# Hybrid HGRN2/Mamba-2 block on one core: the lower parts of 18 weight blocks are made in the stage of step sizes and fetched from DRAM

## The chip, the core and the metric

The kernel runs on 1 core of one Trainium2 chip. The metric is the device time of one execution in microseconds (us), lower is better. Before the change it takes 2316.17 us, the median of 3 runs (2312.27 to 2316.66).

## The reference, cut to what matters

One layer of a hybrid block: a modulated layer norm, two token mixers that read the same input through one combined projection, gates and an output projection, then a feed-forward part. All arrays are float32, with 1024 positions and a width of 1024.

```python
mod = (cond @ w_ada[l] + b_ada[l])[:, None, :]
sh1, sc1, g1, sh2, sc2, g2 = jnp.split(mod, 6, axis=-1)
u = layer_norm(x) * (1.0 + sc1) + sh1
proj = u @ w_in
q, f, i, g, z, xbc, dt, gate_a, gate_b = jnp.split(proj, offs, axis=-1)
y_a = hgrn2_mixer(q, f, i, g, lb, gnorm) @ w_branch_a
y_b = mamba2_mixer(z, xbc, dt, conv_w, conv_b, dt_bias, a_log, d_skip, ssm_norm) @ w_branch_b
...
# in mamba2_mixer
xbc = jax.nn.silu(causal_dwconv(xbc, conv_w, conv_b)).astype(F32)
delta = jax.nn.softplus(dt.astype(F32) + dt_bias.astype(F32)).reshape(bsz, s, B_GROUPS, B_HG)
```

The change concerns the columns of w_in that give xbc: 2048 of x and 4 groups of 128 each for B and C. In the kernel these are 24 weight blocks of 1024 x 128.

## The kernel before, in words

**Two-part products.** A float32 value is split into an upper part (the value cast to a shorter float type, held in 4 bytes) and a lower part (the value less the upper part). A product is three matmuls into the same PSUM bank (`mm`, L80 to L83): lower weights by upper input or the other way round, and upper by upper. The input u stays in SBUF as `uh` and `ul`, in two halves of 512 positions.

**Weight blocks.** `Dense.load` (L67) makes the two parts of one block of 128 x 1024 numbers (512 KB): a transfer on SP's queue into `raw` (L70), a cast to `wh` on ScalarE (L75, called ACT in the profile) and a subtraction to `wl` (L76) on the engine `dn.lo`. That engine is VectorE (DVE) by default and GpSimd (POOL) in the mixers, since `dn.lo = G` is set ahead of each. The tiles `raw`, `wh` and `wl` have two slots each in the pool `wp`, and w_i's pieces (`iraw`) use the slots of `raw` too. So a load waits for the cast and the subtraction of the load two before it, and a `wl` can be written again when TensorE (PE) has ended the block two before. `Dense.unit` (L85) does a block: 2 halves x 8 slices x 3 matmuls, 48 in all, with a bank that is read out after each half.

**Stages around the change.** The stage of step sizes (357 to 467 us) multiplies u by w_i, the 1056 columns of dt and i, in three groups of 352 columns; a group is 8 tiles of 128 positions with 24 matmuls each. Its weights come in four pieces a group (`load_i`, L565) that are split into `iwh` (ScalarE) and `iwl` (VectorE). Beside that it makes four more segments of the modulation (`mod_segment`): 32 pieces `wa` of w_ada (512 KB, L213, three slots) are multiplied by the condition and summed on VectorE into `acc` (L215, L217), and PE reduces `acc` over partitions: 8 products with a column of ones (L222) for two segments, 2 row products (L231) for the other two. `Fill` lets a generator advance to a given step; `mods.to(...)` spreads the 36 steps of the segments over the 24 tiles. `step_sizes` makes delta and its sums on VectorE and ScalarE, and writes them to DRAM as `ac_d`.

Then come the HGRN2 mixer (467 to about 800 us) and the Mamba-2 mixer, in this document "the mixer" (to 1263 us). In the mixer four groups of 8 chunks follow one another. While the chunks of a group are worked on, `dense_x` (L811 on) makes the projection of the next group by `fill`: blocks B, C and 4 blocks of x, each followed by the convolution over 4 taps on VectorE (L832 on full rows, L835 on the 3 columns at an edge). Gate blocks follow behind the last group. A chunk fetches `ac` (L850) and `eb` (L860) from `ac_d`; the group before is normalised by `squares` (it fetches `zs`, L943, multiplies on GpSimd, L944, squares on ScalarE, L946, sums on VectorE, L948) and `finish` (stores `yb_d`, L964).

**What sets the order.** The program's text gives the order in which work is asked for; a scheduler then orders the instructions of each engine by its own estimate of when their operands are ready. Each engine works through its own queue strictly in that order. All transfers named here are issued by one queue, SP's: one that waits (for a slot, or for the data that it stores) holds all behind it.

Of the kernel before, what the change touches and what calls it, by code (L numbers as in the profile page):

```python
# [9 lines left out]
F32 = mybir.dt.float32  # L10
# [22 lines left out]
P = 128  # L33
T = 1024
TT = T // P
# [15 lines left out]

B_Q, B_F, B_G, B_Z, B_X, B_B, B_C, B_GA, B_GB = 0, 8, 16, 24, 40, 56, 60, 64, 72
NBLK = 80

C_CT, C_BADA, C_CW, C_CB, C_DS, C_NW, C_GN, C_LB = 0, 8, 56, 152, 176, 192, 208, 209
NCOL = 225
# [4 lines left out]
class Dense:  # L61
# [2 lines left out]
    def __init__(self, tc, pool, psum):  # L64
        self.nc, self.pool, self.psum, self.lo = tc.nc, pool, psum, tc.nc.vector

    def load(self, src, scale=None, into=None, eng=None):  # L67
        nc = self.nc
        raw = self.pool.tile([P, 1024], F32, tag="raw", name="raw")
        nc.sync.dma_start(out=raw, in_=src)  # L70
        if scale is not None:
            r2 = raw.rearrange("p (k n) -> p k n", k=2)
            nc.vector.tensor_tensor(r2, r2, scale[:, None, :].broadcast_to([P, 2, TH]), op=ALU.mult)
        wh, wl = into or [self.pool.tile([P, 1024], F32R, tag=t, name=t) for t in ("wh", "wl")]
        nc.scalar.copy(wh, raw)  # L75
        (eng or self.lo).tensor_tensor(wl, raw, wh.bitcast(F32), op=ALU.subtract)  # L76
        return wh, wl

# [4 lines left out]
        nc.tensor.matmul(ps, sh, mh, start=False, stop=last)  # L83

    def unit(self, src, uh, ul, evac, ths=(0, 1), fine=False):  # L85
        wh, wl = src if isinstance(src, (tuple, list)) else self.load(src)
        wh = wh.rearrange("p (k n) -> p k n", k=KT)
        wl = wl.rearrange("p (k n) -> p k n", k=KT)
        for th in ths:
            ps = self.psum.tile([P, TH], F32, tag="d", name="dps")  # L90
            for kt in range(KT):
                self.mm(ps, wh[:, kt, :], wl[:, kt, :], uh[th][:, kt, :], ul[th][:, kt, :],
                        kt == 0, kt == KT - 1)
                if fine and kt < KT - 1:
                    yield
            evac(th, ps)
            yield
# [18 lines left out]
def chain(*gens):  # L116
    for g in gens:
        yield from g
# [3 lines left out]
def hybrid_block(ctx, tc, x, w_mod, w_ada, w_blk, w_i, w_ba, w_bb, w_o, w_g, w_u, w_d,  # L122
                 cols, masks, rows, hrows, out):
    nc = tc.nc
# [6 lines left out]
    def act(o, i, func, **k):  # L131

        if table_of[func] != tables[0]:
            tables[0] = table_of[func]
            r = S.preload_act_table_set(tables[0])
            tc.stamp_issue_order_token(r.ins, "act_tables")
        r = S.activation(o, i, func, **k)
        tc.stamp_issue_order_token(r.ins, "act_tables")
# [11 lines left out]
    z_d = tc.dram_tile([16, P, T], F32, name="z_d")  # L150
    h_d = tc.dram_tile([NFT, P, T], F32, name="h_d")
    x1_d = tc.dram_tile([TT, P, D], F32, name="x1_d")

    mk = const.tile([P, NMASK, P], F32, name="mk")
    cl = const.tile([P, NCOL], F32, name="cl")
# [34 lines left out]
    def split(hi, lo, src, eng=G):  # L190
        S.copy(hi, src)  # L191
        eng.tensor_tensor(lo, src, hi.bitcast(F32), op=ALU.subtract)  # L192
# [11 lines left out]
    uh = [bigp.tile([P, KT, TH], F32R, tag="big", name=f"uh{i}") for i in range(2)]  # L204
    ul = [bigp.tile([P, KT, TH], F32R, tag="big", name=f"ul{i}") for i in range(2)]
# [32 lines left out]
    dn = Dense(tc, wp, psd)  # L238

    def gate_evac(which, n, logs=False):  # L240
        dst = (ga_d, gb_d)[which]

        def evac(th, ps):
            sg = wp.tile([P, TH], F32, tag="ge", name="ge")
            if logs:
                act(sg, ps, AF.Exp, scale=-1.0)
                act(sg, sg, AF.Ln, bias=ones[:, 0:1])
                act(sg, sg, AF.Exp, scale=-1.0)
            else:
                act(sg, ps, AF.Sigmoid)  # L250
            nc.sync.dma_start(out=dst[n, :, TH * th:TH * th + TH], in_=sg)
        return evac

    def gate_units(which, n0, n1, fine=False, ths=(0, 1)):
        for n in range(n0, n1):
            yield from dn.unit(w_blk[(B_GA, B_GB)[which] + n], uh, ul, gate_evac(which, n, fine), ths, fine=fine)
# [16 lines left out]
    with tc.tile_pool(name="sw", bufs=1) as sw, tc.tile_pool(name="s0p", bufs=2, space=PSUM) as pp:  # L273
# [176 lines left out]
        for q in range(len(pairs)):  # L450
            blk = pairs[q][0]
# [104 lines left out]
    with tc.tile_pool(name="s1", bufs=2, reuse_waits="tile") as sp, \  # L556
            tc.tile_pool(name="s1p", bufs=2, space=PSUM, reuse_waits="tile") as pp:
        mods = Fill(chain(mod_segment(4, sp, pp, col=3), mod_segment(3, sp, pp, col=2),
                          mod_segment(2, sp, pp, row=0), mod_segment(5, sp, pp, row=1)))
        NI = 352  # L560
        iraw = []

        def load_i(g, k4):
            raw = wp.tile([P, 1024], F32, tag="raw", name="iraw")[:, 0:2 * NI].rearrange("p (k n) -> p k n", k=2)
            nc.sync.dma_start(out=raw, in_=w_i[g, :, 2 * k4:2 * k4 + 2, :])  # L565
            return raw

        bridge = dn.load(w_blk[B_GA + 6])
        iraw = [load_i(0, k4) for k4 in range(2)]
        for g in range(3):  # L570
            wh = sp.tile([P, KT, NI], F32R, tag="iwh", name="iwh")
            wl = sp.tile([P, KT, NI], F32R, tag="iwl", name="iwl")
            for k4 in range(4):
                ks = slice(2 * k4, 2 * k4 + 2)
                raw = iraw.pop(0) if iraw else load_i(g, k4)
                split(wh[:, ks, :], wl[:, ks, :], raw, V if IE[k4] == "V" else G)
            if g == 0:
                for _ in dn.unit(bridge, uh, ul, gate_evac(0, 6), (1,)):
                    pass
                lower_bound()  # L580
            for tt in range(TT):
                ps = psd.tile([P, TH], F32, tag="d", name="dps")
                th, o = tt // 4, P * (tt % 4)
                for kt in range(KT):
                    dn.mm(ps[:, 0:NI], uh[th][:, kt, o:o + P], ul[th][:, kt, o:o + P], wh[:, kt, :], wl[:, kt, :],
                          kt == 0, kt == KT - 1)
                S.copy(i_sb[:, tt, NI * g:NI * g + NI], ps[:, 0:NI])
                mods.to((TT * g + tt + 1 - MO) * 36 / (24 - MO))
                if g == 1 and tt == 4:
                    steps.drain()  # L590
            if g == 0:
                steps = Fill(step_sizes(sp, pp))
                steps.to(1)
        mods.drain()


    def hgrn_phase():
# [208 lines left out]
    def mamba_phase():  # L806
        with tc.tile_pool(name="m", bufs=2, reuse_waits="tile") as mp, \
# [3 lines left out]
            def dense_x(g):  # L811
# [6 lines left out]
                for blk, dst in [(16 + g, bT), (20 + g, cT)] + [(4 * g + j, xT[:, j, :]) for j in range(4)]:  # L818
# [22 lines left out]
                                act(t, t, AF.Silu, bias=cl[:, C_CB + k:C_CB + k + 1])  # L841
                            held[:] = held[1:] if len(held) == 2 and not th else []

                    yield from dn.unit(w_blk[B_X + blk], uh, ul, evac, fine=True)

            def fetch(g, ch):

# [135 lines left out]
            for i in range(N):  # L983
                g, ch = divmod(i, TT)
# [31 lines left out]
    with tc.tile_pool(name="big2", bufs=4, reuse_waits="tile") as big2:  # L1016
        with tc.tile_pool(name="dp", bufs=2, reuse_waits="tile") as dp, \
# [40 lines left out]
            for i, (o, n) in enumerate(steps):  # L1058
                if n == 0:
                    fill = Fill(operand(o + 1) if o < 2 else first_operands())  # L1060
                wh, wl = (t.rearrange("p (k n) -> p k n", k=KT) for t in w)
# [157 lines left out]
        with tc.tile_pool(name="fp", bufs=2, reuse_waits="tile") as fp, \  # L1219
# [139 lines left out]
            for p in range(2):  # L1359
# [10 lines left out]
                into = [None] * 2  # L1370
                if p:
                    ht = [pool.tile([P, 4, 2, TH], F32R, tag=t, name="htl") for pool, t in ((bigp, "big"), (big2, "big2"))]
                    wt = [big2.tile([P, 2, 2, D], F32R, tag="big2", name="wtl") for _ in range(3)]
                    into = [(ht[q // 4][:, q % 4], (wt[q // 2][:, q % 2, 0, :], wt[q // 2][:, q % 2, 1, :])) for q in range(NL)]
# [93 lines left out]
```

## Time and profile before

| | |
|---|---|
| median of 3 runs | 2316.17 us |
| the profiled execution | 2310.18 us |
| its span (first to last instruction) | 2308.4 us |
| mean granted clock of TensorE | 0.988 |
| bytes moved by DMA | 290.75 MB, mean 126 GB/s |

The profile is of one execution. Its first page gives, for each engine, the busy time and its share of the span. Further views list, for a window of time, the busy time of each engine, the clock that TensorE was granted and the load of the 16 DMA engines; for a group of instructions, their number, duration and the idle time ahead of them; for an engine, the waits and what ended each (its releaser). A row of a timeline has the start, the duration, the engine, the line, the operation and, in brackets, the idle time just before it and its releaser. "SPq" is SP's queue of transfers. Matmuls overlap, so one takes longer than the distance from one start to the next.

### The profile page before, as it was taken

To read this page: it belongs to the slowest core of one execution; us is meant where nothing else is said; L and a number is where in the kernel's file an instruction comes from. 1 tells how busy PE (TensorE), PEld (TensorE's weight loads), DVE (VectorE), ACT (ScalarE), POOL (GpSimd) and SP (SyncE) were. 2 spreads that over 40 slices of the span, in tenths; PEclk is the share of its full clock that TensorE was granted. 3 is DMA by queue.
4 is the path that set the end of the run, shared out by engine and by line. 5 is a ranking of instruction groups with operands and counts; after the bars stand their busy time and mean duration, and the time that the engine had idled before them with its cause. 6 is when DMAs were issued, how large, how long until landed. Compare 5 with 4: busy or idle time off the path is not lost.

```text
span 2308.4 us, 32125 instructions
## 1 busy us (share of the span) xinstructions
PE 2230.2 (97%) x12412; PEld 1816.2 (79%) x12412; DVE 1567.8 (68%) x2489; ACT 1061.6 (46%) x1931; POOL 264.8 (11%) x153
## 2 busy tenths in 40 slices
PE   7899999999999999999998999999899999999998
PEld 4778889977777787787776788888788888888886
DVE  5866665638898558898975443468977666653647
ACT  3833333137777646777786320224633333322221
POOL 0000000012222222222231000003400000000000
PEclk9999999999999999999999999999999999999999
DMA  7334326601112312343455643432232222244554
GB/s 282 121 140 136 126 93 209 218 33 52 61 56 69 118 61 92 110 141 115 159 164 183 229 167 102 132 138 95 73 132 101 87 73 92 73 160 151 179 182 132
DMA packets 119649, 290.75 MB, mean 126 GB/s; under 512 B 12101, under 2 KB 26949, under 8 KB 119497
## 3 DMA queue, kind: packets, MB, share of 16 engines
q1 hardware_dynamic: 119496, 288.71, 37.5%
q8 instruction: 97, 1.59, 0.3%
q14 instruction: 56, 0.45, 0.1%
HBM read 235.05 MB, written 53.62 MB: 125 GB/s over the span
## 4 chain that ended last, share of the span: by engine, by line
PE 82%; DVE 8%; ACT 3%; issue 3%; DMA 2%; POOL 2%; SPq 0%; DVEq 0%; POOLq 0%; ACTq 0%
PE dps L81 11%; PE dps L83 11%; PE dps L82 11%; PE fps L81 9%; PE fps L82 9%; PE fps L83 9%; PE dqs L81 4%; PE dqs L83 4%; PE dqs L82 4%; PE hps L83 1%; PE hps L81 1%; PE hps L82 1%; PE sc_ps L701 1%; DVE xTm L832 1%; PE yi L918 1%
## 5 line engine op out<-in xcount | busy, mean ns | idle before, releaser
L81 PE MATMUL dps<-uh,wl 128*128 128x512 f32 x800 | 331.7, 415 | 3.3 <-POOL wl L76 3.3
L83 PE MATMUL dps<-uh,wh 128*128 128x512 f32 x800 | 316.5, 396 | 0.0
L82 PE MATMUL dps<-ul,wh 128*128 128x512 f32 x800 | 314.8, 393 | 0.0
L76 POOL TENSOR_TENSOR wl<-raw,wh 128x1024 fp32r<-128x1024 f32 x49 | 132.1, 2696 | 790.4 <-ACT wh L75 723.4
L81 PEld LDWEIGHTS dps<-uh,wl 128*128 128x128 f32 x800 | 155.1, 194 | 37.6 <-issue 6.6
L83 PEld LDWEIGHTS dps<-uh,wh 128*128 128x128 f32 x800 | 151.9, 190 | 33.8
L82 PEld LDWEIGHTS dps<-ul,wh 128*128 128x128 f32 x800 | 152.5, 191 | 26.7
L81 PE MATMUL dqs<-yp,wl 128*128 128x512 f32 x384 | 147.5, 393 | 6.6 <-ACT yp L191 4.3
L82 PE MATMUL dqs<-yp,wh 128*128 128x512 f32 x384 | 150.4, 392 | 0.0
L83 PE MATMUL dqs<-yp,wh 128*128 128x512 f32 x384 | 150.1, 391 | 0.0
L179 POOL TENSOR_TENSOR mv<-mv,kc 128x1 f32<-128x1 f32 x32 | 32.3, 1015 | 1026.7 <-DVE mv L178 1023.5
L191 ACT CAST cw<-raw 128x512 fp32r<-128x512 f32 x131 | 81.0, 621 | 132.3 <-PE fps L83 87.6
L81 PE MATMUL fps<-t,cw 128*128 128x512 f32 x352 | 137.0, 389 | 0.7 <-DVE cw L192 0.7
L82 PE MATMUL fps<-t,cw 128*128 128x512 f32 x352 | 136.9, 389 | 0.0
L83 PE MATMUL fps<-t,cw 128*128 128x512 f32 x352 | 136.9, 389 | 0.0
L75 ACT CAST wh<-raw 128x1024 fp32r<-128x1024 f32 x76 | 79.6, 1048 | 113.5 <-PE dqs L83 101.8
L192 DVE TENSOR_TENSOR cw<-raw,cw 128x512 fp32r<-128x512 f32 x131 | 94.8, 725 | 43.5 <-ACT cw L191 42.2
L82 PE MATMUL fps<-wl,hp 128*128 128x512 f32 x304 | 118.4, 389 | 0.0
L83 PE MATMUL fps<-wh,hp 128*128 128x512 f32 x304 | 118.3, 389 | 0.0
L192 DVE TENSOR_TENSOR wl<-wdr,wh 128x1024 fp32r<-128x1024 f32 x38 | 46.5, 1224 | 105.4 <-ACT wh L191 105.2
L81 PE MATMUL fps<-wh,hp 128*128 128x512 f32 x304 | 117.0, 390 | 0.5 <-ACT wh L191 0.5
L191 ACT CAST wh<-wdr 128x1024 fp32r<-128x1024 f32 x38 | 40.1, 1054 | 147.4 <-PE fps L83 146.1
(368 smaller groups left out, 5586.4 us busy)
## 6 DMA issues: line engine op xcount, KB each, us to landing
raw<-in_w_blk_dram SPq DMA_DIRECT2D x79, 512.0 KB, 3.4
wdr<-in_w_d_dram SPq DMA_DIRECT2D x44, 512.0 KB, 3.8
wa<-in_w_ada_dram SPq DMA_DIRECT2D x32, 512.0 KB, 4.5
ac<-ac_d SPq DMA_DIRECT2D x32, 512.0 KB, 4.8
raw<-in_w_g_dram SPq DMA_DIRECT2D x26, 512.0 KB, 3.8
raw<-in_w_u_dram SPq DMA_DIRECT2D x26, 512.0 KB, 3.5
hr<-h_d SPq DMA_DIRECT2D x44, 256.0 KB, 3.9
h_d<-sg SPq DMA_DIRECT2D x18, 512.0 KB, 2.9
```

Of the source, the lines that this page charges most:

```text
L75: nc.scalar.copy(wh, raw)
L76: (eng or self.lo).tensor_tensor(wl, raw, wh.bitcast(F32), op=ALU.subtract)
L81: nc.tensor.matmul(ps, sl, mh, start=first, stop=False)
L82: nc.tensor.matmul(ps, sh, ml, start=False, stop=False)
L83: nc.tensor.matmul(ps, sh, mh, start=False, stop=last)
L179: G.tensor_tensor(mv[:, 2:3], mv[:, 1:2], kc[:, 2:3], op=ALU.pow)
L191: S.copy(hi, src)
L192: eng.tensor_tensor(lo, src, hi.bitcast(F32), op=ALU.subtract)
L701: PE.matmul(sp_[b0:b1, 0, b1:b2], lv[c][:, o + b0:o + b1], lv[c][:, o + b1:o + b2], start=True, stop=True)
L832: V.scalar_tensor_tensor(d[:, o:], ps[:, o + j - 3:TH + j - 3], cw(j), d[:, o:], op0=ALU.mult, op1=ALU.add)
L918: PE.matmul(yi[64 * e:64 * e + 64, j, :], xd[:, HP * hh:HP * hh + HP], ac[:, hh, :], start=True, stop=True)
```

## The change

`AHEAD` lists 18 blocks: B, C and the four x of groups 1, 2 and 3. `make_lower` is a generator that loads each of them in the stage of step sizes, splits it (on VectorE there, since `dn.lo` is V) and stores the lower part in the DRAM tile `wl_d`; the store of one block is asked for after the next block's load. A `Fill` spreads the 19 steps over the tiles of the stage's first 22. In the mixer `weights` gives `Dense.unit` a function for these blocks: it loads `raw` and casts it as before, and fetches `wl` from `wl_d` on SP's queue in place of the subtraction. The upper part is not kept. Line numbers move: L70 becomes L71, L76 becomes L80, L213 becomes L218, L565 becomes L587.

```diff
+AHEAD = [b for g in range(1, 4) for b in [B_B + g, B_C + g] + [B_X + 4 * g + j for j in range(4)]]
...
-    def load(self, src, scale=None, into=None, eng=None):
+    def load(self, src, scale=None, into=None, eng=None, lower=None):
...
         nc.scalar.copy(wh, raw)
+        if lower is not None:
+            nc.sync.dma_start(out=wl.bitcast(F32), in_=lower)
+            return wh, wl
         (eng or self.lo).tensor_tensor(wl, raw, wh.bitcast(F32), op=ALU.subtract)
...
-        wh, wl = src if isinstance(src, (tuple, list)) else self.load(src)
+        wh, wl = src() if callable(src) else src if isinstance(src, (tuple, list)) else self.load(src)
...
+    wl_d = tc.dram_tile([len(AHEAD), P, 1024], F32, name="wl_d")
...
+    made = {}
+
+    def weights(blk):
+
+        return (lambda: dn.load(w_blk[blk], lower=wl_d[made[blk]])) if blk in made else w_blk[blk]
+
+    def make_lower(blks):
+
+        last = None
+        for blk in blks + [None]:
+            wl = dn.load(w_blk[blk])[1] if blk is not None else None
+            if last:
+                made[last[0]] = len(made)
+                nc.sync.dma_start(out=wl_d[made[last[0]]], in_=last[1].bitcast(F32))
+            last = blk, wl
+            yield
...
+        lower = Fill(make_lower(AHEAD))
         for g in range(3):
...
                 mods.to((TT * g + tt + 1 - MO) * 36 / (24 - MO))
+                lower.to((TT * g + tt) * (len(AHEAD) + 1) / 22)
...
         mods.drain()
+        lower.drain()
...
-                    yield from dn.unit(w_blk[B_X + blk], uh, ul, evac, fine=True)
+                    yield from dn.unit(weights(B_X + blk), uh, ul, evac, fine=True)
```

The scheduler decides where the new transfers stand. SP's queue at the start of the stage of step sizes, before (`wa`: a piece of w_ada, `iraw`: a piece of w_i, `hr`: constants of the step sizes; the number behind a name is that of the buffer):

```order
L213 DMA wa_2965<-in_w_ada_dram 128x1024
L516 DMA hr_3032<-in_hrows_dram 128x64
L213 DMA wa_2994<-in_w_ada_dram 128x1024
L213 DMA wa_2997<-in_w_ada_dram 128x1024
L213 DMA wa_3026<-in_w_ada_dram 128x1024
L213 DMA wa_3029<-in_w_ada_dram 128x1024
L565 DMA iraw_3059<-in_w_i_dram 128x704
L565 DMA iraw_3063<-in_w_i_dram 128x704
```

And after, from about the same place on (`raw`: a block's load, `wl_d`: the store of a lower part):

```order
L218 DMA wa_2990<-in_w_ada_dram 128x1024
L71 DMA raw_2852<-in_w_blk_dram 128x1024
L71 DMA raw_2884<-in_w_blk_dram 128x1024
L218 DMA wa_2993<-in_w_ada_dram 128x1024
L218 DMA wa_3029<-in_w_ada_dram 128x1024
L272 DMA wl_d_73<-wl_2855 128x1024
L71 DMA raw_2917<-in_w_blk_dram 128x1024
L272 DMA wl_d_73<-wl_2887 128x1024
L71 DMA raw_2957<-in_w_blk_dram 128x1024
L218 DMA wa_3032<-in_w_ada_dram 128x1024
```

Loads and stores of the blocks now stand among the pieces of w_ada; the pieces of w_i for the second group come after seven loads and six stores.

At the end of the stage SP's queue held the following before; the four `raw` are the first weights of the HGRN2 mixer:

```order
L70 DMA raw_3659<-in_w_blk_dram 128x1024
L213 DMA wa_3234<-in_w_ada_dram 128x1024
L213 DMA wa_3237<-in_w_ada_dram 128x1024
L70 DMA raw_3717<-in_w_blk_dram 128x1024
L70 DMA raw_3779<-in_w_blk_dram 128x1024
L70 DMA raw_3886<-in_w_blk_dram 128x1024
L213 DMA wa_3325<-in_w_ada_dram 128x1024
```

Behind these stood 15 more `wa`. After the change the last `wa`, the last store and the same first weights are:

```order
L71 DMA raw_3664<-in_w_blk_dram 128x1024
L272 DMA wl_d_73<-wl_3628 128x1024
L218 DMA wa_3697<-in_w_ada_dram 128x1024
L218 DMA wa_3700<-in_w_ada_dram 128x1024
L272 DMA wl_d_73<-wl_3667 128x1024
L218 DMA wa_3730<-in_w_ada_dram 128x1024
L218 DMA wa_3733<-in_w_ada_dram 128x1024
L232 DMA br_3763<-in_rows_dram 1x1024
L71 DMA raw_3786<-in_w_blk_dram 128x1024
L71 DMA raw_3844<-in_w_blk_dram 128x1024
```

The first weights of the HGRN2 mixer have moved from the middle of the `wa` to behind the last of them.

In the mixer SP's queue held, for about two chunks before (`yb_d`: the store of a group's result; `ac`, `eb`, `zs`: operands of chunks and of the normalisation):

```order
L964 DMA yb_d<-xTm 128x512 x4
L850 DMA ac<-ac_d 128x1024
L70 DMA raw<-in_w_blk_dram 128x1024
L943 DMA zs<-z_d 128x512
L860 DMA eb<-ac_d 64x4x128 x2
L850 DMA ac<-ac_d 128x1024
L943 DMA zs<-z_d 128x512 x3
```

And at the same place after:

```order
L989 DMA yb_d<-xTm 128x512 x4
L875 DMA ac<-ac_d 128x1024
L78 DMA wl<-wl_d 128x1024
L71 DMA raw<-in_w_blk_dram 128x1024
L968 DMA zs<-z_d 128x512
L885 DMA eb<-ac_d 64x4x128 x2
L875 DMA ac<-ac_d 128x1024
L968 DMA zs<-z_d 128x512 x3
```

A fetch of `wl` now stands ahead of the load of `raw`, behind an `ac`.

## The prediction, made before the changed kernel was run

> **What bounds the kernel now.** I read the first page, then busy time by stages, then TensorE's waits in the mixer.
>
> ```profile
> span 2308.4 us, 32125 instructions
> PE 2230.2 (97%) x12412; PEld 1816.2 (79%) x12412; DVE 1567.8 (68%) x2489; ACT 1061.6 (46%) x1931; POOL 264.8 (11%) x153
> ```
>
> PE (TensorE) is busy for 97%, so all its idle time is 78.2 us. A change that adds no matmul can win only some of these, or add to them. The stages that the change touches (columns: window, length, busy time of each engine, clock, DMA share, GB/s):
>
> ```profile
> 357.00:467.00 110.00, 107.80 (x658) 102.31 (x656) 62.78 (x79) 26.69 (x47) 5.22 (x2) 1.00 0.64 212
> 861.00:1059.00 198.00, 190.20 (x1083) 151.11 (x1083) 172.44 (x287) 147.41 (x313) 45.02 (x23) 0.99 0.37 116
> 1059.00:1157.00 98.00, 93.58 (x523) 73.66 (x520) 89.48 (x144) 74.39 (x156) 26.85 (x14) 0.98 0.41 137
> 1157.00:1263.00 106.00, 99.57 (x558) 77.51 (x556) 73.91 (x106) 77.79 (x170) 26.21 (x13) 0.97 0.52 168
> ```
>
> The first row is the stage of step sizes: PE is idle for 2.2 of 110 us, and the DMA moves 212 GB/s at share 0.64, the most of these rows. The others are the mixer from its second group on, idle for 7.8, 4.4 and 6.4 us. TensorE's waits there, by line and releaser (total, times, longest):
>
> ```profile
> PE trx L871 <- ACT xTm L137: 7.4, 2, 4.0
> PE dps L81 <- POOL wl L76: 3.3, 2, 2.4
> PE yi L918 <- ACT csh L191: 3.2, 1, 3.2
> PE yx L910 <- DVE Sm L927: 3.0, 2, 2.5
> ```
>
> Only 3.3 us are waits for a lower part itself. The two waits of trx have the same subtraction some steps back. One of them in order of time:
>
> ```profile
> 1037.90 3.45 POOL L76 TENSOR_TENSOR wl<-raw,wh 128x1024 fp32r<-128x1024 f32 x1 [13.70 <-ACT wh L75]
> 1039.77 1.61 DVE L835 SCALAR_TENSOR_TENSOR xTm<-edge,cl,xTm 128x3 f32<-128x3 f32 x1
> 1041.96 0.20 DVE L835 SCALAR_TENSOR_TENSOR xTm<-edge,cl,xTm 128x3 f32<-128x3 f32 x1
> 1045.40 0.68 DVE L948 TENSOR_TENSOR sqs<-sqs,zs 128x512 f32<-128x512 f32 x1
> 1046.11 1.65 SPq L943 DMA_DIRECT2D zs<-z_d  x2
> 1048.75 1.27 POOL L944 TENSOR_TENSOR xTm<-xTm,zs 128x512 f32<-128x512 f32 x1 [7.40 <-DMA zs<-z_d]
> 1050.06 0.63 ACT L946 ACTIVATE zs<-xTm 128x512 f32<-128x512 f32 x1 [2.62 <-POOL xTm L944]
> 1050.59 0.71 ACT L137 ACTIVATE xTm<-xTm,cl 128x512 f32<-128x512 f32 x1
> 1051.35 0.47 PE L871 MATMUL trx<-mk,xTm 128*128 128x128 f32 x1 [3.98 <-ACT xTm L137]
> ```
>
> A 0.20 us edge operation of VectorE takes 1.61 us and ends only when GpSimd's subtraction ends (1041.35). VectorE is then late with sqs, the fetch of zs waits for sqs, L944 for zs, ScalarE's square for L944, the activation behind it in ScalarE's queue too, and PE stands still for 3.98 us. Then the clock:
>
> ```profile
> 1051.40:1054.50 3.10, 3.10 (x10) 2.62 (x11) 1.91 (x4) 0.86 (x2) 0.00 (x0) 0.50 0.89 227
> 1153.50:1156.90 3.40, 3.40 (x9) 2.65 (x8) 2.22 (x6) 1.94 (x7) 0.00 (x0) 0.50 0.51 160
> ```
>
> After both trx waits PE runs 3.4 us at half clock and loses 1.7 us more each time.
>
> **The mixer, part by part.** Eighteen subtractions leave GpSimd and eighteen fetches of 512 KB join SP's queue.
>
> ```profile
> L76 POOL TENSOR_TENSOR wl<-raw,wh x49: 2339/2423/3464, 410.6 to 1245.0; 128x1024 fp32r<-128x1024 f32 x49
> 966.50 0.50 PE L81 MATMUL dps<-uh,wl 128*128 128x512 f32 x1 [2.36 <-POOL wl L76]
> 1068.38 0.50 PE L81 MATMUL dps<-uh,wl 128*128 128x512 f32 x1 [0.99 <-POOL wl L76]
> 349.93 0.23 PE dps L83
> ```
>
> 18 x 2.42 = 44 us of GpSimd go, but GpSimd sets no end by itself; what PE gets back is this:
>
> - the two waits for wl, both ahead of blocks on the list: 3.3 us, which I count in full;
> - the two trx waits and their half clocks: 7.4 + 2 x 1.7 = 10.8 us. The edge operation loses 1.4 us in the picture above and more before it; other delays in the chain (SP's issues, zs's own landing) stay. Bounds 0 to 10.8; I take two thirds, 7.2, since the delayed operation lies early in a chain where VectorE has no pause.
>
> So the mixer gains 10.5, between 3.3 and 14.1 us. The last two rows of the waits lie after 1157, among gate blocks that are not on the list: 0 for those.
>
> The added fetch waits on SP for the same thing that the subtraction waited for on GpSimd: the wl slot, free when PE ends the block two before. From then PE has a whole block ahead (48 matmuls of 0.23 with mixer work between), over 11 us, and a fetch lands in 3.4 us (below). DMA has 0.37 to 0.41 of its time taken. I count it as hidden; behind it on SP stand raw, eb and ac, which the chunks need. If that cover is gone it is a rival below.
>
> **The stage of step sizes, part by part.** Its queue before and after ends on the modulation's weights wa; PE's last instructions there are the row products of the last segment, which need the last wa.
>
> ```profile
> L213 SPq DMA_DIRECT2D wa<-in_w_ada_dram x32: 327/328/443, 357.1 to 454.6; - x32
> L217 DVE SCALAR_TENSOR_TENSOR acc<-wa,cond,acc x28: 1270/1285/3414, 366.2 to 458.6; 128x1024 f32<-128x1024 f32 x28
> 466.17 0.68 DVE L232 TENSOR_TENSOR br<-mps,br 1x512 f32<-1x512 f32 x1 [6.30 <-PE mps L231]
> wa<-in_w_ada_dram SPq DMA_DIRECT2D x32, 512.0 KB, 4.5
> raw<-in_w_blk_dram SPq DMA_DIRECT2D x79, 512.0 KB, 3.4
> iraw<-in_w_i_dram SPq DMA_DIRECT2D x12, 352.0 KB, 4.1
> L75 ACT CAST wh<-raw x76: 1031/1046/1083, 79.7 to 1512.5; 128x1024 fp32r<-128x1024 f32 x76
> L76 DVE TENSOR_TENSOR wl<-raw,wh x27: 1215/1218/1226, 86.6 to 1513.8; 128x1024 fp32r<-128x1024 f32 x27
> ```
>
> Before: the last acc ends at 459.9 (466.17 less 6.30) and PE reaches its products at 465.2, so the slack is 5.3 us.
>
> Computing is cheap: 18 casts of 1.05 on ScalarE (19 us beside its 26.7 of 110) and 18 subtractions of 1.22 on VectorE (22 beside 62.8). The DMA is not. From the first wa to the last, in MB:
>
> - before: 32 wa x 0.524 + 10 of the 12 iraw x 0.360 + 4 raw x 0.524 = 22.5, in 98 us;
> - after: the 4 raw (weights of the next stage) are pushed behind, 18 raw and 18 stores of wl join: 22.5 - 2.1 + 18.9 = 39.3.
>
> The rates that this stage has reached:
>
> ```profile
> 360.00:370.00 10.00, 9.89 (x59) 9.33 (x58) 6.16 (x13) 4.53 (x8) 0.00 (x0) 1.00 0.96 338
> 357.00:380.00 23.00, 22.89 (x134) 21.80 (x133) 15.13 (x22) 10.11 (x15) 0.00 (x0) 1.00 0.90 305
> 420.00:440.00 20.00, 20.00 (x133) 20.00 (x132) 10.50 (x11) 1.81 (x4) 0.00 (x0) 1.00 0.80 271
> ```
>
> 39.3 MB take 116 us at 338 GB/s, 129 at 305, 145 at 271. From 357.1 the last wa lands at 473, 486 or 502, and with 1.3 us for the last acc PE is let go at 475, 487 or 503 instead of 465.2: 9, **22** or 38 us late. I take 305, the rate of the longest stretch in which the queue was full. 338 would need share 0.96 for 116 us, while all the raw loads share two slots: a load (3.4) with its cast and subtraction (1.05 + 1.22) holds a slot for about 6 us, and SP stands in line behind each.
>
> What else is late: the first weights of the next stage now come after the last wa. One more raw (1.7 us at 305 GB/s), cast 1.05 and GpSimd's 2.4 end about 2 us after PE is through with the products: **+2**. PE has then waited long, so one half clock: **+1.7** (bounds 0 and 5). Waits of PE for iraw in the middle (its loads now stand behind seven raw) are not added: PE would otherwise wait for the same bytes at the end.
>
> The stage loses 22 + 2 + 1.7 = 26 us, bounds 9 and 45.
>
> **Two rules weighed.** The Trainium skill (DMA: Bandwidth & Descriptors, Specifications) gives a core about 358 GB/s of its memory. By that 39.3 MB would take 110 us, an estimate from the page, and the stage would lose about 3 us instead of 22; the trace never held more than 338 over 10 us. The Trainium skill (TensorE: Matmul & The Clock Gate, Part 1) has the clock halve after a window of about 3.4 us without work. By it each stage wait over 3.4 us costs a half-clock stretch; the trace agrees with the two rows at 0.50 above, and I price it from those.
>
> **Sum.** +26 - 10.5 = +15.5. The profiled execution took 2310.18 (span 2308.4 plus 1.8 around it), so 2325.7; the median of the three runs, 2316.17, lies 6.0 above it, which gives **2331 us**. A difference of under 0.2% (4.6 us) can't be told from no change here.
>
> **Rivals.**
>
> 1. *The stage hides it* (faster). The queue never runs dry: 338 GB/s at share 0.96 are 352 at full share, so 39.3 MB take 112 us, PE is let go at 470, 5 us late, too short a wait for a half clock, and the first weights add 2. The mixer gains all of 14.1: 2316 + 7 - 14 = 2309. For it: PE loses only 2.2 us there now, and VectorE and ScalarE have room. Against: mean share 0.64, and two raw slots. Chance 0.15.
> 2. *They cancel*. Rate 338 (9 + 2 + 1.7) against the mixer's 10.5: 2318. Chance 0.13.
> 3. *The fetch becomes the mixer's wait* (slower still). SP does one thing after another: a fetch held behind eb or ac, which wait on VectorE's yt, comes too late, and PE waits a landing (3.4 us). It decides once SP is held for more than 11 - 3.4 = 7.6 us; if a third of 18 are late, 6 x 3.4 = 20 us, and the gain of the trx waits is gone too: 2316 + 26 - 3 + 20 = 2359. Against: SP's queue has a wl about every block, right behind an ac that the same PE releases. Chance 0.07.
> 4. *It doesn't do what it says.* The order shows 18 fetches on SP and 18 fewer subtractions on GpSimd, so none.
>
> My forecast has 0.65, with 2321 to 2348 as its own range. The likeliest is 2331; the range takes the stage from 9 to about 40 and leaves out most of rivals 1 and 3: 2313 to 2349. Slower holds the forecast and rival 3: 0.72. Same 0.13, faster 0.15.
>
> **What would show it.** Right: in the new profile DMA share stays at 0.8 or more through the stage, the last wa lands near 486, PE waits several us for iwl or mps and then for wl of the first block after it, and the start of the next stage moves by 20 to 30 us; in the mixer GpSimd's wl count falls by 18, L835 loses its 1.6 to 2.4 us cases before 1157, and the waits of trx shrink. Wrong: the stage ends within 10 us of 467 (then my rate is wrong), PE's waits of trx stay (then the lock was not their cause), or PE waits for DMA wl in the mixer (rival 3).

## The result, and the profile after

| | before | after |
|---|---|---|
| median of the runs on one chip (4 each) | 2316.24 us | 2330.85 us |
| lowest and highest | 2312.27 to 2316.66 | 2325.72 to 2335.47 |
| the profiled execution, its span | 2310.18, 2308.4 us | 2330.0, 2328.2 us |
| bytes moved by DMA | 290.75 MB | 319.07 MB |

The ratio after to before is 1.0066, interval [1.0042, 1.009]: slower by 14.6 us of the medians. The first page of the profile after:

```profile
span 2328.2 us, 32241 instructions
PE 2237.1 (96%) x12412; PEld 1819.7 (78%) x12412; DVE 1562.1 (67%) x2507; ACT 1079.6 (46%) x1949; POOL 219.2 (9%) x135
```

GpSimd has 18 instructions fewer, VectorE and ScalarE 18 more each, and the matmuls are the same; PE's busy time grew by 6.9 us all the same. The stages, with windows that begin and end at the same matmuls as the windows of before (the first one ends at the first matmul of the HGRN2 mixer, which started at 466.92 before):

```profile
357.00:496.80 139.80, 115.99 (x656) 107.64 (x654) 82.17 (x96) 44.38 (x65) 2.58 (x2) 0.90 0.84 294
894.00:1082.00 188.00, 188.00 (x1083) 150.00 (x1083) 154.33 (x286) 144.61 (x310) 17.08 (x12) 1.00 0.47 153
1082.00:1175.00 93.00, 91.64 (x525) 72.69 (x522) 81.31 (x142) 73.13 (x152) 14.31 (x9) 1.00 0.52 167
1175.00:1281.80 106.80, 99.90 (x557) 77.22 (x556) 74.24 (x109) 79.49 (x175) 26.79 (x13) 0.97 0.51 167
```

The stage of step sizes takes 29.9 us more (496.8 against 466.9), at DMA share 0.84. The three windows of the mixer take 387.8 us where they took 198 + 98 + 106 = 402: 14.2 us less, all of it in the first two, where PE now idles for 0 and 1.4 us. Between the two, in the HGRN2 mixer, the profile after falls another 3.1 us behind, and 1.0 us at the end: 29.9 + 3.1 - 14.2 + 1.0 = 19.8, the difference of the two profiles. TensorE's waits in the stage of step sizes, after (line and releaser; total, times, longest):

```profile
PE dps L85 <- ACT iwh L196: 10.0, 3, 5.2
PE mps L236 <- DVE acc L222: 7.4, 1, 7.4
PE mps L227 <- DVE acc L222: 5.4, 1, 5.4
PE dps L86 <- DVE iwl L197: 0.8, 1, 0.8
```

PE waits for split pieces of w_i (`iwh`, `iwl`) and for sums over w_ada (`acc`), for bytes in most cases. One wait for `iwh`, of 3.46 us at 404.44, follows from the wait for `acc` ahead of it: VectorE stands for `mps`, ScalarE for VectorE's next result, and the cast to `iwh` is behind that in ScalarE's queue. The pieces of w_ada and their sums, in the view by tile (first and last start behind the durations):

```profile
L218 SPq DMA_DIRECT2D wa<-in_w_ada_dram x32: 327/423/1208, 356.5 to 486.0; - x32
L222 DVE SCALAR_TENSOR_TENSOR acc<-wa,cond,acc x28: 1275/1282/1287, 365.6 to 491.9; 128x1024 f32<-128x1024 f32 x28
```

The last piece is issued at 486.0 (454.6 before) and its sum starts at 491.9 (458.6). The end of the stage in order of time, before and then after:

```profile
465.11 1.88 PE L231 MATMUL mps<-acc,mk 128*1 128x512 f32 x4
466.92 0.50 PE L81 MATMUL dps<-uh,wl 128*128 128x512 f32 x1
```

```profile
493.29 3.57 PE L236 MATMUL mps<-acc,mk 128*1 128x512 f32 x4 [7.38 <-DVE acc L222]
496.79 0.70 PE L85 MATMUL dps<-uh,wl 128*128 128x512 f32 x1
```

PE reaches its last row products at 493.29 instead of 465.11. The next stage's first matmul follows at once: no wait for its weights. One stretch in the middle of the stage, in a window of its own:

```profile
394.80:411.90 17.10, 10.21 (x37) 9.67 (x38) 11.17 (x18) 3.73 (x6) 0.00 (x0) 0.50 0.70 233
```

Three waits close together kept PE at half clock for 17 us. In the mixer after, from 894 to 1282, these are the longest of TensorE's waits:

```profile
PE yi L943 <- ACT csh L196: 3.2, 1, 3.2
PE yx L935 <- DVE Sm L952: 3.0, 2, 2.5
PE trx L896 <- ACT xTm L141: 1.4, 1, 1.4
PE cb L898 <- ACT bt L917: 0.4, 1, 0.4
```

No wait for a `wl` is left, and the waits of trx fell from 7.4 to 1.4 us. Those of cb fell too; before they were:

```profile
PE cb L873 <- ACT bt L892: 1.7, 2, 1.5
```

One place shows what had held PE back, because a gate block that is not on the list still does it (after, in order of time):

```profile
1159.34 3.04 POOL L80 TENSOR_TENSOR wl<-raw,wh 128x1024 fp32r<-128x1024 f32 x1 [15.36 <-ACT wh L76]
1159.43 0.68 DVE L959 TENSOR_TENSOR xTm<-xTm,yt 128x512 f32<-128x512 f32 x1
1160.10 0.73 DVE L857 SCALAR_TENSOR_TENSOR xTm<-dps,cl,xTm 128x509 f32<-128x509 f32 x1
1160.76 1.65 DVE L860 SCALAR_TENSOR_TENSOR xTm<-edge,cl,xTm 128x3 f32<-128x3 f32 x1
1162.33 0.73 DVE L857 SCALAR_TENSOR_TENSOR xTm<-dps,cl,xTm 128x509 f32<-128x509 f32 x1
1162.99 0.20 DVE L860 SCALAR_TENSOR_TENSOR xTm<-edge,cl,xTm 128x3 f32<-128x3 f32 x1
```

The edge operation L860 works on 3 columns. It takes 0.20 us once GpSimd is done, but 1.65 while GpSimd subtracts, and it ends with the subtraction (1159.34 + 3.04 = 1162.38). L857, which reads one operand from a bank of PSUM, keeps its 0.73 us at the same time. L959 reads two operands from SBUF and keeps its 0.68; there the subtraction seems to be the one that waits, since it takes 3.04 us in place of its usual 2.40. The Trainium skill (SBUF — State Buffer, Who interferes with whom) has VectorE's instructions with two inputs in SBUF contend with GpSimd's instructions that read SBUF, for a shared port that is an exclusive lock. These rows agree: `edge` and `xTm` are both in SBUF.

### The profile page after: what moved, and what is told of

Read it like the earlier page. It is cut to its first block, busy times and chain, and to the rows that moved or that the text cites. A ratio compares the mean times of both kernels' runs of the same rounds, so it can differ in the third digit from the quotient of the medians.

```text
span 2328.2 us, 32241 instructions
## 1 busy us (share of the span) xinstructions
PE 2237.1 (96%) x12412; PEld 1819.7 (78%) x12412; DVE 1562.1 (67%) x2507; ACT 1079.6 (46%) x1949; POOL 219.2 (9%) x135
## 2 busy tenths in 40 slices
DMA packets 127425, 319.07 MB, mean 137 GB/s; under 512 B 12964, under 2 KB 27812, under 8 KB 127272
## 4 chain that ended last, share of the span: by engine, by line
PE 79%; DVE 9%; ACT 5%; DMA 4%; issue 2%; POOL 1%; SPq 0%; DVEq 0%; ACTq 0%; POOLq 0%
PE dps L85 11%; PE dps L87 10%; PE dps L86 10%; PE fps L85 9%; PE fps L86 9%; PE fps L87 9%; PE dqs L85 4%; PE dqs L87 4%; PE dqs L86 4%; PE hps L87 1%; PE hps L85 1%; PE hps L86 1%; PE yi L943 1%; DMA wa<-in_w_ada_dram 1%; DVE b L663 1%
## 5 line engine op out<-in xcount | busy, mean ns | idle before, releaser
L76 ACT CAST wh<-raw 128x1024 fp32r<-128x1024 f32 x94 | 98.4, 1048 | 133.6 <-PE dqs L87 99.0
L80 POOL TENSOR_TENSOR wl<-raw,wh 128x1024 fp32r<-128x1024 f32 x31 | 85.2, 2749 | 672.9 <-ACT wh L76 614.2
```

## The experiments

All were timed against the kernel before on the same chip. Twelve kernels: five on the cost in the stage of step sizes, seven on the gain in the mixer.

### The two halves of the change

First the making alone (make_lower as in the change, nothing fetched).

```diff
     def weights(blk):
-        return (lambda: dn.load(w_blk[blk], lower=wl_d[made[blk]])) if blk in made else w_blk[blk]
+        return w_blk[blk]
```

> The lower parts are made and stored as in the changed kernel, but nobody fetches them: the mixer subtracts on GpSimd as before. If the stage costs 28 us and the mixer wins 14 independently: about 2316 + 28 + 3 = 2347 us, with PE's stalls of trx and wl back in the mixer. If the mixer's gain in the changed kernel came only from the shifted start (another phase of the queues), it stays and the time is about 2331.

Measured: 2344.08 us against 2317.74, ratio 1.0118 [1.0101, 1.0135], so 26.3 us slower. The mixer's stalls were there again (trx 5.3 us, `wl` 3.9).

Then the fetch alone: no `make_lower`; the bridge block's lower part is stored once, and that one is fetched for all 18.

```diff
-        return (lambda: dn.load(w_blk[blk], lower=wl_d[made[blk]])) if blk in made else w_blk[blk]
+        return (lambda: dn.load(w_blk[blk], lower=wl_d[0])) if blk in AHEAD else w_blk[blk]
...
+        nc.sync.dma_start(out=wl_d[0], in_=bridge[1].bitcast(F32))
```

> The 18 blocks of the mixer fetch one and the same stored block as their lower part, and nothing is made in the stage of step sizes except one extra store there; so the lower parts are not those of the blocks. If the mixer's gain stands by itself: 2316 - 14 = 2302 us, the stage as before. If the gain needs the late start: about 2316. If fetches collide when the start is early: above 2316.

Measured: 2307.67 against 2317.74, ratio 0.9963 [0.995, 0.9976]: 10.1 us faster, between the 2302 and the 2316 that I had written down. In its profile the mixer is as short as after the change (387.9 us between the matmuls that stand 402.0 apart before), so the gain doesn't need the late start. The halves add up, 26.3 - 10.1 = 16.2 against the 14.6 of the change. They can be studied apart.

### Which part of the making costs 26 us

The making without its stores (on the kernel that only makes):

```diff
-                nc.sync.dma_start(out=wl_d[made[last[0]]], in_=last[1].bitcast(F32))
```

> As make-only, but the 18 stores are left out; loads, casts and subtractions stay, the mixer is as before. Bytes theory: 29.9 MB at 303 GB/s are 99 us, less than the stage's 110, so the stage ends within 5 us of before and the time is 2316 to 2322. Chain theory (a slot of raw is held by load, cast and subtraction, and SP stands behind each): the stores were cheap, the loads still hold SP, 15 to 25 us late: 2331 to 2341.

Measured: 2327.11 against 2317.74, ratio 1.0044 [1.003, 1.0059], +9.4 us, between the two theories. Then the loads without cast, subtraction or store:

```diff
-            wl = dn.load(w_blk[blk])[1] if blk is not None else None
+            wl = None
+            if blk is not None:
+                raw = wp.tile([P, 1024], F32, tag="raw", name="raw")
+                nc.sync.dma_start(out=raw, in_=w_blk[blk])
```

> Only the 18 loads are left in the stage (no cast, no subtraction, no store); the mixer is as before. Bytes theory: the same bytes as without the stores, so the same time as that run within 3 us, 2316 to 2322. Chain theory: the slots are now free at landing, so clearly less than without the stores, by 10 us or more.

Measured: 2316.68 against 2317.74, ratio 0.9999 [0.9984, 1.0014]. The 9.4 MB of loads alone are free, and this run is 10.4 us below the one with casts and subtractions, as the chain theory had it. So either the bytes cost nothing until some room is used up and the stores overstep it, or the work on the blocks costs and the stores make it worse by making SyncE stand for VectorE. Two runs bear on this. One moves the change's stores off SyncE's queue:

```diff
-                nc.sync.dma_start(out=wl_d[made[last[0]]], in_=last[1].bitcast(F32))
+                nc.gpsimd.dma_start(out=wl_d[made[last[0]]], in_=last[1].bitcast(F32))
```

> The change, with its 18 stores issued from GpSimd's queue instead of SyncE's; the same bytes move. Theory A, bytes: the stores' 9.4 MB cost the stage their 17 us whichever queue issues them: 2328 to 2334. Theory B, order: the stores cost so much because SyncE stands at each until VectorE has subtracted (42 us in 15 waits) and the loads of weights behind it start late; the loads now go past them, and the stage's 26 us fall towards the 9 of the run without stores: 2312 to 2320.

Measured: 2326.51 against 2317.99, ratio 1.0039 [1.0026, 1.0052], +8.5 us where the change has +14.6. Below Theory A's range, but far from Theory B's: the order in SyncE's queue is worth some 6 us, not 17. The other run moves the bytes of the change without any of its computing:

```diff
-            wl = dn.load(w_blk[blk])[1] if blk is not None else None
+            raw = None
+            if blk is not None:
+                raw = wp.tile([P, 1024], F32, tag="raw", name="raw")
+                nc.sync.dma_start(out=raw, in_=w_blk[blk])
             if last:
                 made[last[0]] = len(made)
-                nc.sync.dma_start(out=wl_d[made[last[0]]], in_=last[1].bitcast(F32))
-            last = blk, wl
+                nc.sync.dma_start(out=wl_d[made[last[0]]], in_=last[1])
+            last = blk, raw
```

> The change's 18 loads and 18 stores of 512 KB in the stage of step sizes, without its casts and subtractions: what is stored is the block as it came, and the mixer makes its lower parts itself, as in the kernel before. Against the run that makes and stores (26.3 us slower than before). Theory A, bytes: the same 39.3 MB at about 303 GB/s put the last piece of w_ada at 486 again: 2336 to 2344. Theory B, order (a slot held through cast and subtraction, SyncE standing at stores for VectorE): only the bytes at the best rate seen are left, and 2318 to 2328 comes out.

Measured: 2342.06 against 2315.94, ratio 1.0116 [1.0099, 1.0134]: +26.1 us without one cast or subtraction, as many as the making costs with them. Its busy times from 357 to 487 (VectorE 58.36 us, against 78.64 in the change):

```profile
357.00:487.00 130.00, 114.54 (x653) 108.10 (x651) 58.36 (x76) 25.23 (x45) 0.00 (x0) 0.92 0.88 308
```

and PE's waits in its stage:

```profile
PE dps L85 <- ACT iwh L196: 10.0, 4, 3.9
PE mps L236 <- DVE acc L222: 5.1, 1, 5.1
PE mps L227 <- DVE acc L222: 3.3, 1, 3.3
PE dps L86 <- DVE iwl L197: 0.4, 2, 0.2
```

The same four waits; those for the sums over w_ada are each about 2 us shorter than in the change (7.4 and 5.4 there). What this run takes away is the computing alone. SyncE still stands at the stores, now for the block to land (34.7 us in 16 waits, where it stood 42.5 us in 15 for VectorE in the change), and a slot of `raw` is now held until its store has been read from it.

The runs side by side, 357 to 487 us (GB/s and DMA share over these 130 us; in the first three rows the stage is over before the window ends). The last column but one is the start of the HGRN2 mixer's first matmul in each profile:

| run | joins the queue | GB/s | DMA share | last wa issued | next stage starts | time against before |
|---|---|---|---|---|---|---|
| before | nothing | 185 | 0.56 | 454.6 | 466.9 | |
| loads alone | 9.4 MB | 258 | 0.74 | 458.2 | 468.4 | -1.1 |
| loads, casts, subtractions | 9.4 MB | 254 | 0.73 | 465.7 | 474.0 | +9.4 |
| loads and stores, no computing | 18.9 MB | 308 | 0.88 | 481.8 | 493.9 | +26.1 |
| all of the making | 18.9 MB | 301 | 0.86 | 485.7 | 496.0 | +26.3 |
| the change | 18.9 MB | 300 | 0.86 | 486.0 | 496.8 | +14.6, with the mixer's gain |
| the change, stores on GpSimd's queue | 18.9 MB | 313 | 0.90 | 482.6 | 493.2 | +8.5, with the mixer's gain |

So it is the loads and stores that set the end of the stage, not the computing. Half of the bytes fit into the room that was there. Without computing, or with the stores out of SyncE's queue, the last `wa` is issued only some 4 us earlier, and in both runs the DMA engines are busy for 0.88 to 0.90 of the time. That this share is itself the limit is argued from these figures; no run frees the queue, the slots and the engines of computing all at once. With casts and subtractions, which hold the two `raw` slots longer, the loads come out 9 us slower than before; in the profiles 5.6 us of that (474.0 against 468.4) lie in the stage itself. These are not added to the 26 us of the loads and stores.

### What the mixer's gain hangs on

Theory A: GpSimd's subtractions hold VectorE's edge operations. Theory B: PE, or a copy for it, waits for the lower part itself. First, the fetch alone plus a GpSimd subtraction whose result nobody reads:

```diff
         if lower is not None:
             nc.sync.dma_start(out=wl.bitcast(F32), in_=lower)
+            nc.gpsimd.tensor_tensor(raw, raw, wh.bitcast(F32), op=ALU.subtract)
             return wh, wl
```

> The kernel with the fetch alone, plus one GpSimd subtraction for each of the 18 blocks, of the size of the one that the fetch replaced, into the raw slot, whose result nobody reads (the fetched lower part is one stored block for all 18, so the output is not the reference's). Theory A, GpSimd's work: the mixer's 10 to 14 us go away because GpSimd no longer runs beside VectorE's copies, whose single instructions took 1.4 to 2.4 us then. With the 18 subtractions back beside them the stalls come back: 2315 to 2319 us, within 2 us of the kernel before, and copies of 1.4 us or longer are in the trace again. Theory B, what waits for the lower part: the stalls went because PE, or the copies that it waits for, no longer wait for a subtraction to end; nobody waits for these, so the time stays at that of the fetch alone, 2306 to 2309.

Measured: 2319.75 against 2315.21, ratio 1.0012 [1.0, 1.0024]. The gain of the fetch is gone although no engine reads what is subtracted (only the next load waits for the slot, as it does before the change). Its groups of instructions from 861 to 1263 (count | busy us, mean ns), edge operations of VectorE first, then the spare subtractions:

```profile
L846 DVE SCALAR_TENSOR_TENSOR xTm<-edge,cl,xTm 128x3 f32<-128x3 f32 x39 | 17.1, 437 | 0.0
L846 DVE SCALAR_TENSOR_TENSOR cT<-edge,cl,cT 128x3 f32<-128x3 f32 x9 | 5.3, 588 | 0.0
L79 POOL TENSOR_TENSOR raw<-raw,wh 128x1024 f32<-128x1024 f32 x17 | 43.7, 2570 | 132.6 <-ACT wh L76 97.4 <-issue 25.3 <-DVE yt L942 9.8
```

Operations of 0.20 us take 0.44 and 0.59 in the mean. The same groups of the kernel before, and then of the run with the fetch alone:

```profile
L835 DVE SCALAR_TENSOR_TENSOR xTm<-edge,cl,xTm 128x3 f32<-128x3 f32 x36 | 19.4, 538 | 0.0
L835 DVE SCALAR_TENSOR_TENSOR cT<-edge,cl,cT 128x3 f32<-128x3 f32 x9 | 7.0, 775 | 0.0
```

```profile
L845 DVE SCALAR_TENSOR_TENSOR xTm<-edge,cl,xTm 128x3 f32<-128x3 f32 x39 | 11.6, 297 | 0.0
L845 DVE SCALAR_TENSOR_TENSOR cT<-edge,cl,cT 128x3 f32<-128x3 f32 x9 | 1.9, 213 | 0.0
```

Next, the kernel before with the 18 subtractions on VectorE, and no fetch:

```diff
-                    yield from dn.unit(w_blk[B_X + blk], uh, ul, evac, fine=True)
+                    yield from dn.unit((lambda: dn.load(w_blk[B_X + blk], eng=V)) if B_X + blk in AHEAD else w_blk[B_X + blk], uh, ul, evac, fine=True)
```

> The kernel before with the same 18 subtractions of the mixer on VectorE in place of GpSimd; nothing is made ahead, stored or fetched. Theory A, GpSimd's work: VectorE pays some 1.2 us for each block in place of copies that were held for up to 2.4 us, and PE waits for no subtraction that runs 2.4 us: 2304 to 2312. Theory B, what waits for the lower part: VectorE's queue gets 18 times 1.2 us (22 us), part of it ahead of the copies on which PE waits, and the stalls stay or grow: 2316 to 2325.

Measured: 2308.72 against 2315.21, ratio 0.9974 [0.9961, 0.9988]: faster, although VectorE, the busiest engine beside PE there, got 18 subtractions more. That is Theory A's outcome. Its waits from 861 to 1263 that concern a lower part:

```profile
PE dps L82 <- DVE wl L77: 6.6, 3, 3.0
```

The waits of trx for `xTm` are gone. Three for VectorE's subtraction have come; two more runs load each block half a block earlier, with the subtraction on VectorE and on GpSimd:

```diff
+            order = [b for g in range(GB) for b in [16 + g, 20 + g] + [4 * g + j for j in range(4)]]
+            early = {}
...
-                    yield from dn.unit(w_blk[B_X + blk], uh, ul, evac, fine=True)
+                    at = order.index(blk) + 1
+                    for n, _ in enumerate(dn.unit(early.pop(blk, w_blk[B_X + blk]), uh, ul, evac, fine=True)):
+                        if n == 7 and 6 <= at < len(order):
+                            early[order[at]] = dn.load(w_blk[B_X + order[at]], eng=V)
+                        yield
```

(on GpSimd without `eng=V`)

> The kernel before with the 18 subtractions of the mixer on VectorE, as in the run before with VectorE, and each of these blocks loaded, cast and subtracted half a block earlier (behind the first half's copies of the block ahead of it); nothing made ahead, stored or fetched. In the run without the earlier load PE still waited for VectorE's subtraction three times in the mixer, 6.6 us in all. If those three waits are the subtraction's place in VectorE's queue, they go and nothing else changes: 2301 to 2305. If VectorE's added work is what is late (22 us in its queue), the waits move to the copies: 2307 to 2312.

> The same earlier load of the 18 blocks, but with the subtractions left on GpSimd: of the two causes it takes away only that PE waits for a subtraction itself. By the theory that GpSimd's work holds VectorE's copies, those stalls stay (9 to 11 us of the 14 in the mixer): 2311 to 2317. If what waits for the lower part is the cause, the whole gain comes: 2304 to 2308.

Measured on VectorE: 2301.52 against 2317.99, ratio 0.9924 [0.991, 0.9938], the fastest of all. On GpSimd: 2322.73, ratio 1.002 [1.0012, 1.0029], slower than before and above the range that I had given for Theory A. Of PE's waits from 861 to 1263, these concern lower parts and trx on VectorE:

```profile
PE dps L81 <- DVE wl L76: 1.3, 2, 1.0
```

and on GpSimd there is no wait for a lower part, but these:

```profile
PE trx L877 <- ACT xTm L137: 8.6, 3, 4.2
PE cb L879 <- ACT bt L898: 2.8, 2, 1.5
PE dps L81 <- DVE cT L837: 1.7, 2, 1.0
PE dps L81 <- DVE xTm L837: 0.8, 1, 0.8
```

With the earlier load PE waits for a subtraction for 1.3 us on VectorE and not at all on GpSimd, and yet the run on GpSimd is slower. There the subtraction falls on more of VectorE's edge operations (those on `xTm` take 0.69 us in the mean), and PE waits for what these delay. Theory A holds for the stalls of trx, by this pair of runs. Theory B's waits exist beside it, but are the smaller part: 3.3 us before the change. The first page of the run on VectorE:

```profile
span 2300.6 us, 32116 instructions
PE 2231.4 (97%) x12412; PEld 1816.7 (79%) x12412; DVE 1562.6 (68%) x2507; ACT 1061.4 (46%) x1931; POOL 220.6 (10%) x135
```

VectorE has 18 instructions more than before, worth 18 x 1.22 = 22 us, and is busy for 5.2 us less (1567.8 before): the time that it was held had been counted as busy. The largest group of operations on rows of 512 that became shorter reads two operands from SBUF too (before, then here; count | busy us, mean ns):

```profile
L934 DVE TENSOR_TENSOR xTm<-xTm,yt 128x512 f32<-128x512 f32 x32 | 32.5, 1015 | 0.3
L940 DVE TENSOR_TENSOR xTm<-xTm,yt 128x512 f32<-128x512 f32 x32 | 23.2, 725 | 0.2
```

### Fewer blocks

Two kernels make only some of the blocks, in order to have the gain without the cost:

```diff
-AHEAD = [b for g in range(1, 4) for b in [B_B + g, B_C + g] + [B_X + 4 * g + j for j in range(4)]]
+AHEAD = [B_B + 2, B_X + 11, B_B + 3, B_X + 15]
```

> The change with four blocks in place of 18: those whose subtractions stood right ahead of the removed stalls of 2.4, 5.7, 1 and 5.1 us (the block of B and the last block of x for groups 2 and 3). The cost of making, if it goes with the number of blocks: 26.3 x 4 / 18 = 6 us; if the stage has room for four because its transfers have slack (18 loads alone cost nothing): 0 to 2. The gain, if the stalls hang on these four: 10 to 13; if other blocks' subtractions then hit the same copies: 3 to 6. Together 2304 to 2308 where both go well, 2313 to 2319 where neither does.

> The change with ten blocks in place of 18: the block of B and the four of x for groups 2 and 3. The cost of making, by the number of blocks: 26.3 x 10 / 18 = 14.6; if it begins only where the transfers' slack is used up (the loads alone cost nothing, and stores of half the bytes would be 8.5 of 17): 4 to 9. The gain by the stalls that went in the change's trace behind 960: 10 to 13. By number of blocks 2318 to 2322; by slack 2309 to 2316.

Measured: with four blocks 2311.36 against 2315.21, ratio 0.9979 [0.9966, 0.9992]; with ten (`[b for g in (2, 3) for b in [B_B + g] + [B_X + 4 * g + j for j in range(4)]]`) 2312.95, ratio 0.9987 [0.9973, 1.0]. The cost did not go with the number of blocks: the last piece of w_ada was issued at 457.1 and 460.5, so both fitted into the room. The gain was small because I had read only some of the right blocks off the trace. With four blocks the waits of trx fell as hoped, from 7.4 to 0.8 us, but PE still waits in the mixer for lower parts, for 6.6 us where it was 3.3:

```profile
PE dps L85 <- POOL wl L80: 6.6, 2, 3.3
```

for two subtractions that come right after fetches of B's block and of x's:

```profile
966.75 2.37 POOL L80 TENSOR_TENSOR wl<-raw,wh 128x1024 fp32r<-128x1024 f32 x1
1066.99 2.36 POOL L80 TENSOR_TENSOR wl<-raw,wh 128x1024 fp32r<-128x1024 f32 x1
```

They are those of block C of groups 2 and 3, which stand at 964.11 and 1065.91 before and were on neither list. A list with these two in it was not tried.

## Why the prediction was right, step by step

**The direction and the total** were right: 2331 us forecast, 2330.85 measured. That they meet within 0.2 us is luck: the four runs of the change lie between 2325.72 and 2335.47. Against the medians of the two halves both large terms are close (25.7 forecast and 26.3 measured for the making, 10.5 and 10.1 for the mixer); against the two profiles both are some 4 us too small, with opposite signs.

**Bytes in the stage.** 39.3 MB at 305 GB/s put the last `wa` at 486; it was issued at 486.0, at 300 GB/s. That the loads and stores are the cause, and not the computing, is now shown by the run that moves them without it. My second limit, loads that hold a slot, is real (+9.4 alone) but lies beside it. The rule of the Trainium skill that I weighed (DMA: Bandwidth & Descriptors, Specifications: about 358 GB/s) would have given 3 us. Single stretches of 10 us did reach it (360 GB/s from 470 to 480 us of the change), but the best rate over the 130 us was 313 GB/s, at share 0.90, with the stores on another queue.

**From the last piece to PE.** I had let PE go at 487, 1.3 us behind the last `wa`. This step was mis-sized: 98 us was the time from the first issue to the last, so 486 is an issue too and not a landing. The sum started 5.9 us later (491.9), PE's products at 493.29: 28.2 us late, not 22.

**First weights of the next stage, +2.** Nothing: no wait stands ahead of the matmul at 496.79. GpSimd's first subtraction ran from 494.22 to 496.57, beside the products. Had these run at full clock, PE would have waited for it, so this term and the next overlap and should not have been added.

**Half clock, +1.7.** The four products took 496.79 - 493.29 = 3.5 us instead of 466.92 - 465.11 = 1.8: +1.7, as forecast. The 3.4 us that I weighed as the wait that brings half clock are not a bound in these traces: before the change PE ran at clock 0.50 from 1221.8 to 1225.1 after a wait of 2.46 us, though not after one of 2.36 (at 966). The long half-clock stretch in the middle was not in my sum and did not need to be: with its waits it was covered, as I had said of the waits for iraw, because the last bytes set the end anyway. 28.2 + 0 + 1.7 = 29.9 against my 25.7.

**Mixer, -10.5.** 14.2, at my upper bound of 14.1. Both waits for `wl` went, as counted. For the trx waits and their half clocks two thirds was too little: 6.0 of 7.4 us and both half clocks (3.4 us) went. The waits of cb, which I had not counted, gave 1.3 more: 3.3 + 6.0 + 3.4 + 1.3 = 14.0. One reading was wrong. The second trx wait (3.43 us before) stands behind a subtraction of the first gate block (1139.43), which is not on the list. That subtraction and the edge operation that it holds are still there after the change, and so are 1.4 us of the wait; which removed subtraction took the other 2 us, the rows don't say. The mechanism, the held edge operation at the head of a chain, is shown by the spare subtraction (gain gone) and by VectorE's own (gain there). By medians the gain is 10.1 us; I can't tell which of the two is nearer.

**The added fetch hidden.** Right: 18 fetches land in 5.0 us in the median, and PE waits for none. Rival 3 did not come, nor did 1 and 2: the queue held 300 GB/s over the stage, not 338.

**From the profile to the median, +6.0.** This failed as a step between the profiles. I took over that the profiled execution before lies 6.0 below the median; the one after lies only 0.9 below its own, and the two profiles differ by 19.8 us, not by 15.5. The medians differ by 14.6. The profile of before is an early one: three kernels that leave the stage of step sizes as it was (subtractions on VectorE, and the two with the earlier load) start the HGRN2 mixer at 472.0, 468.6 and 470.7, where it has 466.9. So up to 5 of the 29.9 us may be a matter of the execution. The profile after has 3.1 us more in the HGRN2 mixer too, where nothing changed. Some runs that don't touch that part show the same creep (the loads alone: 1.5 us behind at its start, 2.9 at its end) and some don't (the earlier load on VectorE: 1.6 and 1.4). All 15 executions of before beside the first four experiments lie above its profile, at 2313.78 to 2323.03, and of the 75 beside all experiments three lie below. What makes an execution differ by these few us stays open.

## What to carry to other kernels

Count the bytes that a stage can still take before its last transfer is late: here 9.4 MB of loads were free, and as many bytes of stores on top of them cost 26 us, with or without the computing (at 300 GB/s they take 31). Before work is moved away from GpSimd at a price, see whom it holds: an instruction of VectorE that takes many times its usual 0.2 us is the sign, and the cheapest cure was to give the work to VectorE itself, half a block early (2301.5 us, no byte moved), though VectorE looked like the busier engine.

## What the runs showed of the hardware

A held instruction does not appear as idle time but as a longer instruction, so VectorE's busy share hides it; with 18 more instructions it became less busy. It goes both ways: GpSimd's subtraction, 2.40 us in most rows, took 3.45 where an operation of VectorE was ahead of it. With loads and stores of 512 KB mixed, the DMA engines stayed at 300 to 313 GB/s over 130 us; the median landing of a piece of w_ada rose from 4.5 to 6.1 us.
